# GDN gates held in their SBUF buffers until the mLSTM gate adds them, and rows of x asked for one step sooner

## The chip, the cores and the metric

The kernel runs on one core of a Trainium2 chip. Five engines work side by side, each through its own queue in order: TensorE (PE, whose weight loads are shown apart as PEld), VectorE (DVE), ScalarE (ACT), GpSimd (POOL) and SyncE (SP), which issues the DMAs here. The metric is the device time in microseconds. Three runs of the kernel before took 1170.3, 1171.71 and 1173.52 us; the median, 1171.71, is the time before.

## The reference

One decoder layer with two groups of heads side by side, for a prompt of 1024 tokens (behind 16 learned meta tokens) and 8 sample tokens with cached state; D_MODEL is 1024:

```python
# x <- x + W_out [ mLSTM_group(h) ; GDN_group(h) ],  h = RMSNorm(x)
# all head inputs from one projection h @ W_in; every branch has a SiLU gate path;
# a final RMSNorm is applied
M_HEADS, M_DK, M_DV = 4, 128, 256       # mLSTM, matrix memory
G_HEADS, G_DK, G_DV = 8, 128, 128       # gated DeltaNet
```

Outputs are the rows y for prompt and sample, and the new states of both groups. What the change touches is the end of it: each head's result (normalised, in 128-wide pieces, eight of the mLSTM group and eight of the GDN group) is multiplied by its gate and enters the product with W_out, whose result is added to x.

## The kernel before, in words

**Stages.** First come the projections and the chunked recurrences. Each head's normalised result is left in DRAM as `h_d[k]`, 128 x 1024 per piece: k = 0 to 7 are mLSTM pieces and 8 to 15 GDN heads. The gate values z of the GDN heads stand in `g_d`. From about 800 us on TensorE computes the gates of the mLSTM pieces: for j = 0 to 7 one job `o{j}` and one `zm{j}`, each in three blocks of 344 columns (in texts: o1_0, o1_1, o1_2, zm1_0 ...) of 24 matmuls (three for each of eight slices of D: high by high, low by high, high by low). A block goes to one of two PSUM banks in turn. An o block is emptied by a tanh on ScalarE (`to`), a zm block by a tanh on ScalarE (`thzm`) and two operations on VectorE (`mg<-thzm,pjzm`, which frees the bank, and `mg<-to,mg`). Splits of weights into high and low parts run between (`who`, `whzm` on ScalarE, `wlo`, `wlzm` on VectorE).

**Gates.** Both kinds of gate are one generator, `gate` (L1691). For a GDN piece (number 8 + j) it loads y from `g_d` and ht from `h_d`, multiplies them (`y<-ht,wgh,y`, four operations on VectorE), stores y to `y_d` in DRAM, makes the high and low part of its first half for the left operand of the first output product (`left<-y`, `left<-y,left`), and stores the difference of its halves in `s_d`. For mLSTM piece j it loads ht, multiplies it with the gate mg (`mg<-ht,wmq,mg`, four operations), loads the y of GDN piece j back from `y_d` as `yg`, forms two sums (`ht<-mg,yg`), another sum and a difference (`yg<-yg,mg`, `yg<-mg`), and stores five pieces in `c_d`. Buffers come from the ring `r_gm`, which has five here; `r_gm.can()` says whether one is free.

**Output products.** The product with W_out is done as seven products (`out_products`), 0 to 6, of sums and differences of halves (a scheme of Strassen's kind: s_d and c_d hold the left sums, `owh`/`owl` the right ones). Each has four banks t = 0 to 3 and steps k = 0 to 7, 96 matmuls of 512 columns; product p begins a bank when the drain of product p - 2 has emptied it. A drain (`drain`) adds a bank to the rows of x, which it finds in the buffers `regionxl` (three pieces) and `xr1_1`, `xr0_2`, `xr1_2`, `xr0_3`, `xr1_3`. `residual` (L2059) asks for these rows from DRAM; `("used", p, k)` is noted when product p's step k has been written for its last bank.

**Order.** A planner (`Plan`) sets the order of the work. Each part of the program is a generator that yields what it waits for; the planner keeps an estimated clock per engine and estimated times at which tiles are written and read, takes the next part by them and records the instruction on its engine. All instructions are recorded by one helper, so that every row of the profile shows L56. The sample tokens' head (`small`, `mqT`, `mqc`, `wb`, `mms`) is woven between the gate jobs by the same planner: `mqT` turns a row on TensorE, `mqc` are its small products, after which GpSimd multiplies two 128 x 1024 states by a decay (`small<-small,sgb`), the six `wb` operations of 8 elements are its weights, and `mms` begins a chain of some twenty operations of 32 elements (`wb`, ending in `hs`), a Newton iteration for its norm.

Of the kernel before, what the change touches and what calls it, by code (L numbers as in the profile page):

```python
# [12 lines left out]
F32 = mybir.dt.float32  # L13
# [294 lines left out]
def hymba_kernel(ctx: ExitStack, tc: tile.TileContext, a: dict, o: dict):  # L308
# [1365 lines left out]
    y_d = dr.tile([GH, P, SEQ], F32, name="y_d")  # L1674
    s_d = dr.tile([GH, P, HALF], F32, name="s_d")
    c_d = dr.tile([GH, P, 5, HALF], F32, name="c_d")
    for t, size in ((y_d, P * SEQ), (s_d, P * HALF), (c_d, 5 * P * HALF)):
        plan.split(t, size)
# [12 lines left out]
    def gate(kt_, wcol):  # L1691

        j = kt_ % 8
        if kt_ >= 8:
            yield lambda: ("mP", MH - 1) in done and ("H", kt_) in done and ("z", j) in done and (j in slots or (r_kq if j < 6 else r_N).can()) and r_gm.can(2)
            gi, y = r_gm.get([SEQ], f"y{kt_}")
        else:
            yield lambda: ("H", kt_) in done and ("y", 8 + j) in done and (j < 2 or ("y", j - 2) in done) and r_gm.can()
        hi, ht = r_gm.get([8, P], f"ht{kt_}")
        yield max(plan.read[ht.tensor.name], plan.read[y.tensor.name] if kt_ >= 8 else 0.0)  # L1700
        if kt_ >= 8:
            sp.dma_start(y, g_d[j])
        sp.dma_start(ht.rearrange("p c t -> p (c t)"), h_d[kt_])
        yield ht
        if kt_ < 8:
            yield has("zm", j)
            gi, y = hd["mg", j]
        yield y
        if kt_ < 8:
            act.activation(gs[:, j, :], y[:, SEQ:NO], AF.Copy, scale=wcol)  # L1710
        u = ht.rearrange("p c t -> p (c t)")
        for a_ in range(4):
            yield "dve"
            to = y[:, 0:SEQ].rearrange("p (c a i) -> p a c i", c=8, a=4)[:, a_]
            dve.scalar_tensor_tensor(out=to, in0=u[:, 256 * a_ : 256 * a_ + 256].rearrange("p (c i) -> p c i", c=8), scalar=wcol, in1=to, op0=ALU.mult, op1=ALU.mult)
        yield y
        if kt_ >= 8:
            sp.dma_start(y_d[j], y)
            high, low = slot(j)
            act.copy(high, y[:, 0:HALF])  # L1720
            dve.tensor_tensor(out=u[:, 0:HALF], in0=y[:, HALF:SEQ], in1=y[:, 0:HALF], op=ALU.subtract)
            yield high
            dve.tensor_tensor(out=low, in0=y[:, 0:HALF], in1=high.bitcast(F32), op=ALU.subtract)
            r_gm.free(gi)
            yield u
            sp.dma_start(s_d[j], u[:, 0:HALF])
            r_gm.free(hi)
        else:
            sp.dma_start(c_d[j, :, 0], y[:, HALF:SEQ])
            yield r_gm.can  # L1730
            yi, g = r_gm.get([SEQ], f"yg{j}")
            yield plan.read[g.tensor.name]
            sp.dma_start(g, y_d[j])
            yield g
            for half in (slice(0, HALF), slice(HALF, SEQ)):
                yield "dve"
                dve.tensor_tensor(out=u[:, half], in0=y[:, half], in1=g[:, half], op=ALU.add)
            yield "dve"
            dve.tensor_tensor(out=g[:, 0:HALF], in0=g[:, 0:HALF], in1=y[:, HALF:SEQ], op=ALU.add)
            yield "dve"  # L1740
            dve.tensor_tensor(out=g[:, HALF:SEQ], in0=y[:, 0:HALF], in1=y[:, HALF:SEQ], op=ALU.subtract)
            r_v.free(gi)
            yield g
            sp.dma_start(c_d[j, :, 1:3], u.rearrange("p (a t) -> p a t", a=2))
            r_gm.free(hi)
            sp.dma_start(c_d[j, :, 3:5], g.rearrange("p (a t) -> p a t", a=2))
            r_gm.free(yi)
# [544 lines left out]
```

## Time and profile before

| | |
|---|---|
| median of three runs | 1171.71 us (1170.3 to 1173.52) |
| the profiled execution, in all | 1170.97 us |
| its span, first to last instruction | 1169.2 us |
| mean granted TensorE clock | 0.998 |
| PE / PEld / DVE / ACT / POOL busy | 1151.9 / 1079.4 / 910.6 / 587.8 / 467.6 us |
| DMA | 171.63 MB, mean 147 GB/s |

In timelines a row has start, duration (of one, or over a group xN), engine, line, operation, out<-in, shape, and in brackets the idle time before it with what ended it. In the table of stretches a row has the stretch, its length, busy time (and instructions) of PE, PEld, DVE, ACT and POOL, the granted clock, the DMA engines' share and GB/s. Matmuls overlap in the pipeline: one of 344 columns lasts 0.32 us in a row, and the next starts 0.157 us after it. A wait's row names the waiting engine and tile, the engine and tile that ended the wait, the total, the count and the longest.

### The profile page before, as it was taken

The page shows a single profiled execution, that of the slowest core. Times are in us where ns is not written, and L with a number is a line of the kernel's source. Part 1 is how long each engine was busy: PE and PEld are TensorE (multiplying, and loading weights), DVE is VectorE, ACT ScalarE, POOL GpSimd, SP SyncE. Part 2 cuts the span into 40 slices and gives each one's busy share as a digit, 9 for nine tenths or more (in the row PEclk, how much of TensorE's full clock was granted, in tenths as well). Part 3 has the DMA queues.
Part 4 walks back from the last instruction along what each step waited for, and adds up shares of the span by engine and source line. Part 5 has one row for each costly group of instructions (what it writes and reads, how often), then busy time and mean ns, then how long its engine had stood idle before and what let it go on. Part 6 is the DMA issues. An engine that isn't in the chain of part 4 may idle for free.

```text
span 1169.2 us, 22728 instructions
## 1 busy us (share of the span) xinstructions
PE 1151.9 (99%) x8049; PEld 1079.4 (92%) x8049; DVE 910.6 (78%) x2324; ACT 587.8 (50%) x1814; POOL 467.6 (40%) x644
## 2 busy tenths in 40 slices
PE   8999999999999999999999999999999999999997
PEld 7999999999999999999999998999999999876885
DVE  6789878698787879887664967677877765997896
ACT  6544445565655565745454546466532222433443
POOL 3104877855738285958411451311111000530012
PEclk9999999999999999999999999999999999999999
DMA  6032311322121223022423294677998888673342
GB/s 249 18 100 71 95 51 50 102 60 88 46 83 62 81 64 88 26 67 83 120 79 107 70 338 142 244 236 252 297 361 284 303 296 312 214 263 121 107 155 88
DMA packets 94461, 171.63 MB, mean 147 GB/s; under 512 B 28026, under 2 KB 53842, under 8 KB 94347
## 3 DMA queue, kind: packets, MB, share of 16 engines
q1 hardware_dynamic: 94152, 170.01, 44.2%
q8 instruction: 63, 1.03, 0.3%
q14 instruction: 52, 0.42, 0.1%
q10 hardware_dynamic: 194, 0.17, 0.0%
HBM read 116.04 MB, written 54.10 MB: 146 GB/s over the span
## 4 chain that ended last, share of the span: by engine, by line
PE 85%; DMA 6%; DVE 5%; issue 2%; ACT 1%; SPq 1%; POOL 0%; DVEq 0%; ACTq 0%
PE pjg L56 24%; PE pjm L56 15%; PE op L56 9%; PE pjz L56 8%; PE pjo L56 5%; PE pjzm L56 4%; PE up L56 4%; PE tp L56 3%; PE sk L56 2%; PE mnm L56 2%; PE mup L56 2%; PE kk L56 1%; DMA out_s_C<-small 1%; DMA s_d<-ht 1%; DMA ht<-h_d 1%
## 5 line engine op out<-in xcount | busy, mean ns | idle before, releaser
L56 PE MATMUL pjg<-xht,whg 128*128 128x350 f32 (+6 forms) x624 | 197.4, 323 | 1.0 <-ACT xht L56 1.0
L56 PE MATMUL pjg<-xlt,whg 128*128 128x350 f32 (+6 forms) x624 | 196.8, 322 | 0.0
L56 PE MATMUL pjg<-xht,wlg 128*128 128x350 f32 (+6 forms) x592 | 190.3, 325 | 0.0
L56 POOL TENSOR_TENSOR tmp<-B,E 33x31 f32<-33x31 f32 (+15 forms) x248 | 146.2, 590 | 70.9 <-DMA B<-nd 52.1
L56 POOL TENSOR_TENSOR E<-E,tmp 33x31 f32<-33x31 f32 (+15 forms) x248 | 155.5, 627 | 19.4
L56 PE MATMUL op<-owh,left 128*128 128x512 f32 x448 | 141.5, 395 | 2.4 <-DVE xr L56 2.4
L56 PE MATMUL pjm<-xht,whm 128*128 128x350 f32 (+2 forms) x384 | 127.1, 331 | 0.0
L56 PE MATMUL pjm<-xht,wlm 128*128 128x350 f32 (+2 forms) x384 | 126.4, 329 | 0.0
L56 PE MATMUL pjm<-xlt,whm 128*128 128x350 f32 (+2 forms) x384 | 125.4, 327 | 0.0
L56 PEld LDWEIGHTS pjg<-xht,whg 128*128 128x128 f32 x624 | 116.4, 189 | 1.6 <-issue 1.2
L56 PEld LDWEIGHTS pjg<-xlt,whg 128*128 128x128 f32 x624 | 116.4, 189 | 0.4
L56 PEld LDWEIGHTS pjg<-xht,wlg 128*128 128x128 f32 x592 | 110.9, 189 | 0.5
L56 PEld LDWEIGHTS op<-owh,left 128*128 128x128 f32 x448 | 84.1, 188 | 24.8 <-DVE xr L56 3.3
L56 DVE SCALAR_TENSOR_TENSOR kq<-cr,prm,kq 128x346 f32<-128x346 f32 (+7 forms) x147 | 97.2, 667 | 10.8 <-ACT cr L56 8.0
L56 PE MATMUL op<-owl,left 128*128 128x512 f32 x224 | 88.5, 395 | 0.0
L56 PEld LDWEIGHTS pjm<-xht,wlm 128*128 128x128 f32 x384 | 72.4, 189 | 0.5 <-issue 0.2
L56 PEld LDWEIGHTS pjm<-xht,whm 128*128 128x128 f32 x384 | 72.4, 188 | 0.5 <-issue 0.2
L56 PEld LDWEIGHTS pjm<-xlt,whm 128*128 128x128 f32 x384 | 72.4, 188 | 0.5 <-issue 0.2
L56 ACT COPY cr<-pjg 128x3 f32<-128x3 f32 (+8 forms) x124 | 40.5, 327 | 51.3 <-PE pjg L56 50.9
L56 PE MATMUL pjo<-xht,who 128*128 128x344 f32 x192 | 61.9, 322 | 2.3 <-ACT to L56 1.5
L56 PE MATMUL pjz<-xht,wlz 128*128 128x344 f32 x192 | 62.8, 327 | 0.0
L56 PE MATMUL pjz<-xht,whz 128*128 128x344 f32 x192 | 62.8, 327 | 0.0
(377 smaller groups left out, 3095.3 us busy)
## 6 DMA issues: line engine op xcount, KB each, us to landing
wrg<-in_wt SPq DMA_DIRECT2D x23, 512.0 KB, 3.6
left<-c_d SPq DMA_DIRECT2D x40, 256.0 KB, 2.7
wrm<-in_wt SPq DMA_DIRECT2D x16, 512.0 KB, 6.0
h_d<-turn SPq DMA_DIRECT2D x64, 128.0 KB, 3.9
ht<-h_d SPq DMA_DIRECT2D x16, 512.0 KB, 9.3
gm<-rows_d SPq DMA_DIRECT2D x8, 576.0 KB, 5.5
xt<-in_x_p SPq DMA_DIRECT2D x8, 512.0 KB, 5.0
wrz<-in_wt SPq DMA_DIRECT2D x8, 512.0 KB, 3.3
```

Source lines behind the costliest of these rows:

```text
L56: r = f(*args, **kw)
```

## The change

GDN gates and mLSTM gates become two generators that share `scaled`. A GDN gate no longer stores y to DRAM; it keeps its buffer in `hd["y", j]`, and the mLSTM gate of the same number takes it from there, forms the sums in it, and frees it after the store to `c_d`. A GDN gate from number 2 on now starts only when the mLSTM gate two numbers earlier is done, a condition that stood on the mLSTM gate before. `y_d` is gone, with its eight stores and eight loads. In `residual` the rows of x for t = 2 are asked for when product 1 has used step 0 (before: step 1), and those for t = 3 when it has used step 1 (before: step 2).

```diff
--- before.py
+++ after.py
@@ -1671,10 +1671,9 @@
     ys = gp.tile([P, 20, NS], F32, name="ys")
     wgh = gp.tile([P, 1], F32, name="wgh")
     wmq = gp.tile([P, 8], F32, name="wmq")
-    y_d = dr.tile([GH, P, SEQ], F32, name="y_d")
     s_d = dr.tile([GH, P, HALF], F32, name="s_d")
     c_d = dr.tile([GH, P, 5, HALF], F32, name="c_d")
-    for t, size in ((y_d, P * SEQ), (s_d, P * HALF), (c_d, 5 * P * HALF)):
+    for t, size in ((s_d, P * HALF), (c_d, 5 * P * HALF)):
         plan.split(t, size)
     slots = {}
     def slot(k):
@@ -1688,64 +1687,64 @@
                 slots[k + i] = t[:, i, 0], t[:, i, 1]
         return slots[k]
 
-    def gate(kt_, wcol):
-
-        j = kt_ % 8
-        if kt_ >= 8:
-            yield lambda: ("mP", MH - 1) in done and ("H", kt_) in done and ("z", j) in done and (j in slots or (r_kq if j < 6 else r_N).can()) and r_gm.can(2)
-            gi, y = r_gm.get([SEQ], f"y{kt_}")
-        else:
-            yield lambda: ("H", kt_) in done and ("y", 8 + j) in done and (j < 2 or ("y", j - 2) in done) and r_gm.can()
-        hi, ht = r_gm.get([8, P], f"ht{kt_}")
-        yield max(plan.read[ht.tensor.name], plan.read[y.tensor.name] if kt_ >= 8 else 0.0)
-        if kt_ >= 8:
-            sp.dma_start(y, g_d[j])
-        sp.dma_start(ht.rearrange("p c t -> p (c t)"), h_d[kt_])
-        yield ht
-        if kt_ < 8:
-            yield has("zm", j)
-            gi, y = hd["mg", j]
-        yield y
-        if kt_ < 8:
-            act.activation(gs[:, j, :], y[:, SEQ:NO], AF.Copy, scale=wcol)
-        u = ht.rearrange("p c t -> p (c t)")
+    def scaled(y, ht, wcol):
+
         for a_ in range(4):
             yield "dve"
             to = y[:, 0:SEQ].rearrange("p (c a i) -> p a c i", c=8, a=4)[:, a_]
-            dve.scalar_tensor_tensor(out=to, in0=u[:, 256 * a_ : 256 * a_ + 256].rearrange("p (c i) -> p c i", c=8), scalar=wcol, in1=to, op0=ALU.mult, op1=ALU.mult)
+            h_ = ht[:, 256 * a_ : 256 * a_ + 256].rearrange("p (c i) -> p c i", c=8)
+            dve.scalar_tensor_tensor(out=to, in0=h_, scalar=wcol, in1=to, op0=ALU.mult, op1=ALU.mult)
         yield y
-        if kt_ >= 8:
-            sp.dma_start(y_d[j], y)
-            high, low = slot(j)
-            act.copy(high, y[:, 0:HALF])
-            dve.tensor_tensor(out=u[:, 0:HALF], in0=y[:, HALF:SEQ], in1=y[:, 0:HALF], op=ALU.subtract)
-            yield high
-            dve.tensor_tensor(out=low, in0=y[:, 0:HALF], in1=high.bitcast(F32), op=ALU.subtract)
-            r_gm.free(gi)
-            yield u
-            sp.dma_start(s_d[j], u[:, 0:HALF])
-            r_gm.free(hi)
-        else:
-            sp.dma_start(c_d[j, :, 0], y[:, HALF:SEQ])
-            yield r_gm.can
-            yi, g = r_gm.get([SEQ], f"yg{j}")
-            yield plan.read[g.tensor.name]
-            sp.dma_start(g, y_d[j])
-            yield g
-            for half in (slice(0, HALF), slice(HALF, SEQ)):
-                yield "dve"
-                dve.tensor_tensor(out=u[:, half], in0=y[:, half], in1=g[:, half], op=ALU.add)
+
+    def gdn_gate(j):
+
+        yield lambda: ("mP", MH - 1) in done and ("H", 8 + j) in done and ("z", j) in done and (j in slots or (r_kq if j < 6 else r_N).can()) and r_gm.can(2) and (j < 2 or ("y", j - 2) in done)
+        gi, y = r_gm.get([SEQ], f"y{8 + j}")
+        hi, u = r_gm.get([SEQ], f"ht{8 + j}")
+        yield max(plan.read[u.tensor.name], plan.read[y.tensor.name])
+        sp.dma_start(y, g_d[j])
+        sp.dma_start(u, h_d[8 + j])
+        yield u
+        yield y
+        yield from scaled(y, u, wgh)
+        high, low = slot(j)
+        act.copy(high, y[:, 0:HALF])
+        dve.tensor_tensor(out=u[:, 0:HALF], in0=y[:, HALF:SEQ], in1=y[:, 0:HALF], op=ALU.subtract)
+        yield high
+        dve.tensor_tensor(out=low, in0=y[:, 0:HALF], in1=high.bitcast(F32), op=ALU.subtract)
+        yield u
+        sp.dma_start(s_d[j], u[:, 0:HALF])
+        r_gm.free(hi)
+        hd["y", j] = gi, y
+        done.add(("y", 8 + j))
+
+    def gate(j, wcol):
+
+        yield lambda: ("H", j) in done and ("y", 8 + j) in done and r_gm.can()
+        hi, u = r_gm.get([SEQ], f"ht{j}")
+        yield plan.read[u.tensor.name]
+        sp.dma_start(u, h_d[j])
+        yield u
+        yield has("zm", j)
+        (vi, y), (gi, g) = hd["mg", j], hd["y", j]
+        yield y
+        act.activation(gs[:, j, :], y[:, SEQ:NO], AF.Copy, scale=wcol)
+        yield from scaled(y, u, wcol)
+        sp.dma_start(c_d[j, :, 0], y[:, HALF:SEQ])
+        for half in (slice(0, HALF), slice(HALF, SEQ)):
             yield "dve"
-            dve.tensor_tensor(out=g[:, 0:HALF], in0=g[:, 0:HALF], in1=y[:, HALF:SEQ], op=ALU.add)
-            yield "dve"
-            dve.tensor_tensor(out=g[:, HALF:SEQ], in0=y[:, 0:HALF], in1=y[:, HALF:SEQ], op=ALU.subtract)
-            r_v.free(gi)
-            yield g
-            sp.dma_start(c_d[j, :, 1:3], u.rearrange("p (a t) -> p a t", a=2))
-            r_gm.free(hi)
-            sp.dma_start(c_d[j, :, 3:5], g.rearrange("p (a t) -> p a t", a=2))
-            r_gm.free(yi)
-        done.add(("y", kt_))
+            dve.tensor_tensor(out=u[:, half], in0=y[:, half], in1=g[:, half], op=ALU.add)
+        yield "dve"
+        dve.tensor_tensor(out=g[:, 0:HALF], in0=g[:, 0:HALF], in1=y[:, HALF:SEQ], op=ALU.add)
+        yield "dve"
+        dve.tensor_tensor(out=g[:, HALF:SEQ], in0=y[:, 0:HALF], in1=y[:, HALF:SEQ], op=ALU.subtract)
+        r_v.free(vi)
+        yield g
+        sp.dma_start(c_d[j, :, 1:3], u.rearrange("p (a t) -> p a t", a=2))
+        r_gm.free(hi)
+        sp.dma_start(c_d[j, :, 3:5], g.rearrange("p (a t) -> p a t", a=2))
+        r_gm.free(gi)
+        done.add(("y", j))
 
     def silu_evac(name, g, to=None):
         def evac(pt, c0, n):
@@ -1811,7 +1810,7 @@
 
     def gdn_gates():
         for h in range(GH):
-            yield from gate(8 + h, wgh)
+            yield from gdn_gate(h)
 
     def gate_jobs():
         def tile_(key, name):
@@ -2060,7 +2059,7 @@
         yield has("region")
         for h in (1, 0):
             for t in range(4):
-                yield has("used", 2 - h, t - (t > 1) if h else t)
+                yield has("used", 2 - h, t // 3 if h else t)
                 for c in range(2):
                     if h:
                         n = 2 * t + c
```

The planner's order is the same on all engines up to about the block zm0_1. Three places where it differs follow, as the queues stand.

VectorE around the evacuation of the block zm0_2 (`pjzm0_2` is its bank, `y9`/`ht9` GDN gate 9, `ebuf` and `wb` the sample head). Before:

```order
L56 SCALAR_TENSOR_TENSOR mg0_10741<-thzm0_360_10852,pjzm0_1_10805 128x344
L56 SCALAR_TENSOR_TENSOR mg0_10741<-to0_10372,mg0_10741 128x344
L56 TENSOR_TENSOR wlo1_10815<-wro1_10338,who1_10814 128x256
L56 SCALAR_TENSOR_TENSOR y9_10735<-ht9_10736,wgh_166,y9_10735 128x8x32 x4
L56 SCALAR_TENSOR_TENSOR ebuf0_101<-ebuf1_102,wb_105,ebuf0_101 128x128 x2
L56 SCALAR_TENSOR_TENSOR mg0_10741<-thzm0_704_10897,pjzm0_2_10856 128x344
```

And now:

```order
L56 SCALAR_TENSOR_TENSOR mg0_10738<-thzm0_360_10856,pjzm0_1_10803 128x344
L56 SCALAR_TENSOR_TENSOR mg0_10738<-to0_10371,mg0_10738 128x344
L56 TENSOR_TENSOR wlo1_10813<-wro1_10337,who1_10812 128x256
L56 SCALAR_TENSOR_TENSOR y9_10733<-ht9_10734,wgh_166,y9_10733 128x8x32 x2
L56 TENSOR_TENSOR wb_105<-mqT0_10851,sgb_97 128x8
L56 TENSOR_TENSOR wb_105<-wb_105,msam_160 128x8
L56 TENSOR_TENSOR wb_105<-wb_105 128x8
L56 TENSOR_TENSOR wb_105<-mqT0_10851,sgb_97 128x8
L56 TENSOR_TENSOR wb_105<-wb_105,msam_160 128x8
L56 TENSOR_TENSOR wb_105<-wb_105 128x8
L56 SCALAR_TENSOR_TENSOR y9_10733<-ht9_10734,wgh_166,y9_10733 128x8x32 x2
L56 SCALAR_TENSOR_TENSOR mg0_10738<-thzm0_704_10921,pjzm0_2_10860 128x344
```

The six `wb` operations have moved in ahead of the evacuation: on TensorE `mqT` now stands between zm0_1 and zm0_2 and `mqc` behind 12 matmuls of zm0_2, where before both stood in o1_1.

VectorE around the sample head's Newton chain, with `mms` on TensorE (before in o5_1, now in o4_2 behind 12 of its 24 matmuls). Before:

```order
L56 SCALAR_TENSOR_TENSOR wb<-mms,wb 128x32
L56 TENSOR_SCALAR wb<-wb 128x32
L56 TENSOR_TENSOR wb<-wb 128x32 x2
L56 TENSOR_SCALAR wb<-wb 128x32
L56 TENSOR_TENSOR wb<-wb 128x32
L56 TENSOR_TENSOR wlzm_12041<-wrzm_11837,whzm_12040 128x384
L56 TENSOR_TENSOR wb<-wb 128x32 x2
L56 TENSOR_SCALAR wb<-wb 128x32
L56 TENSOR_TENSOR wb<-wb 128x32
L56 TENSOR_TENSOR wlzm_12041<-wrzm_11837,whzm_12040 128x384
```

And now, from the chain's end on:

```order
L56 TENSOR_TENSOR wb<-wb 128x32 x3
L56 TENSOR_SCALAR wb<-wb 128x32
L56 TENSOR_TENSOR wb<-wb 128x32
L56 TENSOR_TENSOR hs<-wb 128x4x8 x2
L56 SCALAR_TENSOR_TENSOR mg_11600<-ht_11729,wmq,mg_11600 128x8x32 x3
L56 TENSOR_TENSOR ht_11729<-mg_11600,y_11477 128x512 x2
L56 TENSOR_TENSOR y_11477<-y_11477,mg_11600 128x512
L56 TENSOR_TENSOR y_11477<-mg_11600 128x512
L56 SCALAR_TENSOR_TENSOR mg_11888<-thzm_16_11922,pjzm_0_11889 128x344
```

The chain has no weight splits in it any more; three products and four sums of mLSTM gate 3 follow it, and then the evacuation of zm4_0.

VectorE in the drains of products 0 and 1 (`op0_3` is product 0's bank 3). Before:

```order
L56 TENSOR_TENSOR xr1_2_12904<-xr1_2_12904,op0_2_12701 128x512
L56 TENSOR_TENSOR regionxl_12684<-regionxl_12684,op1_0_12852 128x512
L56 TENSOR_TENSOR xr1_1_12900<-xr1_1_12900,op1_1_12861 128x512
L56 TENSOR_TENSOR xr0_3_12922<-xr0_3_12922,op0_3_12705 128x512
L56 TENSOR_TENSOR left2_11101<-left2_11101 128x512
L56 TENSOR_TENSOR xr1_3_12924<-xr1_3_12924,op0_3_12705 128x512
```

And now:

```order
L56 TENSOR_TENSOR xr1_2_12858<-xr1_2_12858,op0_2_12678 128x512
L56 TENSOR_TENSOR left0_10693<-left0_10693 128x512
L56 TENSOR_TENSOR xr0_3_12879<-xr0_3_12879,op0_3_12682 128x512
L56 TENSOR_TENSOR owl0_12565<-regionxl_12661,owh0_12564 128x512 x2
L56 TENSOR_TENSOR xr1_3_12881<-xr1_3_12881,op0_3_12682 128x512
L56 TENSOR_TENSOR regionxl_12661<-regionxl_12661,op1_0_12831 128x512
L56 TENSOR_TENSOR xr1_1_12854<-xr1_1_12854,op1_1_12836 128x512
```

Both drains of bank 3 of product 0 now stand ahead of two drains of product 1 and of a split of a left slot (`left2`).

## The prediction

> **What bounds the kernel now.** I read the busy shares first, then TensorE's waits over the stretch in which the change acts, then the three stretches as a table.
>
> ```profile
> span 1169.2 us, 22728 instructions
> PE 1151.9 (99%) x8049; PEld 1079.4 (92%) x8049; DVE 910.6 (78%) x2324; ACT 587.8 (50%) x1814; POOL 467.6 (40%) x644
> ...
> PE op L56 <- DVE xr L56: 2.4, 2, 2.0
> PE pjo L56 <- ACT to L56: 1.5, 1, 1.5
> PE pjo L56 <- DVE mg L56: 0.8, 1, 0.8
> PE pjzm L56 <- DVE mg L56: 0.2, 1, 0.2
> ...
> 800.00:1000.00 200.00, 197.42 (x1312) 192.74 (x1311) 149.75 (x374) 71.60 (x206) 23.97 (x11) 1.00 0.86 300
> 1000.00:1045.00 45.00, 42.56 (x183) 33.64 (x182) 43.90 (x51) 16.91 (x30) 21.14 (x8) 1.00 0.73 257
> ```
>
> TensorE is busy for all but 17.3 of 1169.2 us. From 780 us to the end its waits (the four rows; total us, times, longest) come to 2.4 + 1.5 + 0.8 + 0.2 = 4.9 us, and the rest of its idle time lies before that stretch and behind its last matmul, which the change leaves alone. No matmul is removed. So 4.9 us, 0.42% of the span, is all that can be won, whatever is taken off the queues. The window rows (PE, PEld, DVE, ACT, POOL, clock, DMA share, GB/s) show where slack is thin: DMA engines 86% busy in the gate stretch, VectorE 43.90 of 45 us busy in the drains.
>
> The five waits have two kinds of cause. Three are in the gate stretch, the two long ones of which are these:
>
> ```profile
> 952.54 1.67 DVE L56 SCALAR_TENSOR_TENSOR y<-ht,wgh,y 128x256 f32<-128x256 f32 x4 [4.71 <-DMA ht<-h_d]
> 955.28 0.43 PE L56 MATMUL pjo<-xht,who 128*128 128x344 f32 x1 [1.52 <-ACT to L56]
> 968.74 1.67 DVE L56 SCALAR_TENSOR_TENSOR y<-ht,wgh,y 128x256 f32<-128x256 f32 x4 [3.56 <-DMA ht<-h_d]
> 971.36 0.42 PE L56 MATMUL pjo<-xht,who 128*128 128x344 f32 x1 [0.76 <-DVE mg L56]
> ```
>
> VectorE waits 4.71 us for a GDN gate's state. ScalarE's cast of that gate's y waits for VectorE, and the tanh that empties a projection bank (to) is queued behind the cast, so TensorE loses 1.52. The next wait is 3.56 and costs 0.76. In both places TensorE forgives about 3 us (4.71 - 1.52 = 3.19; 3.56 - 0.76 = 2.80) and then pays one for one. The other two waits are in the first two output products:
>
> ```profile
> 1041.18 0.50 PE L56 MATMUL op<-owh,left 128*128 128x512 f32 x1 [0.41 <-DVE xr L56]
> 1043.44 1.27 DVE L56 TENSOR_TENSOR xr<-xr,op 128x512 f32<-128x512 f32 x2
> 1044.17 0.50 PE L56 MATMUL op<-owh,left 128*128 128x512 f32 x1 [2.03 <-DVE xr L56]
> ```
>
> Product 2 needs the banks of product 0, whose last drain VectorE finishes in the x2 group at 1043.44 (0.60 us apiece), too late by 2.03.
>
> **The change part by part.** First the round trip through DRAM.
>
> ```profile
> y_d<-y SPq DMA_DIRECT2D x8, 512.0 KB, 3.7
> yg<-y_d SPq DMA_DIRECT2D x8, 512.0 KB, 5.5
> ...
>   DMA yg<-y_d: 6.9, 3
> ```
>
> Sixteen transfers of 512 KB go, 8.4 MB; all eight pairs sit between 800 and 1015 us, where 300 GB/s times 200 us is 60 MB, so about a seventh of that stretch's traffic. VectorE loses three waits of 6.9 us together (the last row, from the tile yg). None of those three is at one of the five places where TensorE waits, so they give nothing directly. They give room on VectorE. No vector, scalar or GpSimd operation is added or removed; SP issues 16 fewer.
>
> For the gate-phase waits, 1.52 + 0.76 + 0.18 = 2.46 us: the state loads have a seventh less traffic against them, which speaks for their going. Against it: a GDN gate's buffer is now held until the mLSTM gate of its number has stored its sums, so the loads of gates 12 to 15 stand behind stores out of the very buffers that they fill, where before the first store released them. Bounds: all 2.46 gained, or none. I take 1.5, so that 1.0 stays: the traffic is sure to go, and the release has room in the mean (the held buffers, below).
>
> The drain waits, 0.41 + 2.03 = 2.44 us: product 0's last drain moves ahead of three other vector operations, 3 x 0.60 = 1.8 us, and an idle piece in front of the last gate goes:
>
> ```profile
> 1014.24 0.69 DVE L56 TENSOR_TENSOR ht<-mg,yg 128x512 f32<-128x512 f32 x1 [0.93 <-DVE owl L56]
> ...
> 1024.84 2.23 SPq L56 DMA_DIRECT2D xr<-in_x_p  x3
> ...
> 1029.38 0.99 SPq L56 DMA_DIRECT2D xr<-in_x_p  x2
> ```
>
> 1.8 + 0.93 = 2.7 us, more than the 2.03 and the 0.41. The rows of x asked for one k step sooner cost nothing: two DMA groups move up in SP's queue past one weight load, and there is no new transfer. With the old times they were issued at 1024.84 and 1029.38 and wanted from about 1038 on, so their own lateness isn't a term; what they do is let the planner write the drains earlier. Bounds: all 2.44, or none if VectorE, 98% busy there, only trades one late operation for another. I take all.
>
> Now what the new order puts in the way. The sample head's turning and its mqc products move from the block o1_1 into zm0_2 on TensorE; with them six small wb operations move in among gate 8's, and GpSimd's pair of products starts there.
>
> ```profile
> 823.16 0.32 PE L56 MATMUL pjzm<-xht,whzm 128*128 128x344 f32 x1
> 826.92 0.32 PE L56 MATMUL pjo<-xht,who 128*128 128x344 f32 x1
> 831.94 0.60 PE L56 MATMUL mqT<-ident,srow 128*128 128x128 f32 x4
> 834.35 1.08 PE L56 MATMUL mqc<-small,msam 128*32 128x128 f32 x32
> 835.11 4.11 POOL L56 TENSOR_TENSOR small<-small,sgb 128x1024 f32<-128x1024 f32 x2 [14.90 <-PE mqc L56]
> 835.56 1.81 DVE L56 TENSOR_TENSOR wb<-wb,msam 128x8 f32<-128x8 f32 x1
> 837.40 1.84 DVE L56 TENSOR_TENSOR wb<-wb 128x8 f32<-128x8 f32 x1
> ```
>
> While GpSimd runs its two 2.05 us products, a vector operation with two operands in SBUF waits for the end of one of them: 1.81 and 1.84 us for what takes 0.16 otherwise (the row at 900.02, below). About one gets through per product. Placed in zm0_2: the block starts at 823.16; the turning (0.60) and 12 matmuls of 0.157 ((826.92 - 823.16)/24) bring mqc to 825.6; GpSimd starts 0.76 later (834.35 to 835.11), 826.4, and ends at 826.4 + 4.11 = 830.5. VectorE's queue then:
>
> ```profile
> 826.39 0.42 DVE L56 TENSOR_TENSOR wlo<-wro,who 128x256 fp32r<-128x256 f32 x1
> 826.72 1.67 DVE L56 SCALAR_TENSOR_TENSOR y<-ht,wgh,y 128x256 f32<-128x256 f32 x4
> 828.83 0.51 DVE L56 SCALAR_TENSOR_TENSOR mg<-thzm,pjzm 128x344 f32<-128x344 f32 x1
> ...
> 900.02 0.16 DVE L56 TENSOR_TENSOR wb<-mqT,sgb 128x8 f32<-128x8 f32 x1
> 900.70 1.78 DVE L56 TENSOR_TENSOR wb<-wb 128x8 f32<-128x8 f32 x1
> ```
>
> After wlo and one y product have got through, three y products (3 x 0.40) and the six wb (900.02 to 0.17 past 900.70, 0.85 when free) are left: 830.5 + 1.2 + 0.85 = 832.55, and the evacuation of zm0_2 (0.51) ends at 833.1. TensorE reaches o1_1, which wants that bank, at 826.92 + 0.60 + 1.08 (mqc) + 24 x 0.157 = 832.4; before, it got there at 830.7, and the evacuation had ended at 829.3. A new stall of 0.7, and 0.3 of hand-over: 1.0 us. Bounds: 0 where the operations don't collide, and 2.0 where one more y product is left (0.4) and GpSimd starts later, or TensorE's insertions take less than their rows (0.6).
>
> The Trainium skill, "SBUF — State Buffer", section Who interferes with whom, has a vector operation with two SBUF inputs blocked fully by a GpSimd operation that reads SBUF, and one with a single SBUF input not held at all. By that the evacuation, which reads PSUM too, isn't itself held, and the stall comes only from what is queued before it, as in the sum; if it were held as well, the stall would be the same, since its turn comes after 830.5. The rows at 835.56 and 837.40 agree with the blocking.
>
> The second place is the Newton chain for the sample's norms. Before, it stood among weight splits in o5_1; now it stands in o4_2 in one piece, and three mg products and four gate sums follow it, ahead of the evacuation of zm4_0.
>
> ```profile
> 928.04 0.53 PE L56 MATMUL mms<-wb,ones 128*128 128x32 f32 x4
> 928.61 0.19 DVE L56 SCALAR_TENSOR_TENSOR wb<-mms,wb 128x32 f32<-128x32 f32 x1 [1.40 <-PE mms L56]
> 928.83 1.99 DVE L56 TENSOR_SCALAR wb<-wb 128x32 int32<-128x32 int32 x1
> 934.23 0.29 DVE L56 TENSOR_TENSOR hs<-wb 128x32 f32<-128x32 f32 x2
> ...
> 862.17 1.29 DVE L56 TENSOR_TENSOR ht<-mg,yg 128x512 f32<-128x512 f32 x2 [1.93 <-DMA yg<-y_d]
> ```
>
> From the start of mms: 0.57 to the chain, the chain 5.9 less two splits of 0.47 = 5.0 (a blocked 1.99 in it), products 1.2, sums 2.5 (two in 1.29), evacuation 0.5, hand-over 0.2: 10.0 us. TensorE wants the bank after mms 0.5, 12 matmuls 1.9, and two blocks 7.5: 9.9. So 0.1 late with the blocked piece in it and 1.7 early without; bounds 0 and 1.9 (one more blocked operation). I take 0.4.
>
> Sum: -2.4 - 1.5 + 1.0 + 0.4 = -2.5 us. The profiled execution took 1170.97 in all (1.8 around its span); 1170.97 - 2.5 = 1168.5. The runs' median of 1171.71 lies 0.74 above that execution, so 1169.2 on the runs' terms.
>
> **The rivals.** *All old waits go, no new one comes:* -4.9, 1166.1 on the profiled execution, 1166.8 on the median. For it: less traffic, no added work. Against it: the two new places above have no cover left by their own rows.
>
> *Slower, the held buffers:* GDN gates 12 to 15 load only after a store from their buffer has landed, and VectorE's queue is in order, with the evacuations of two banks behind each y product. It decides once VectorE waits more than about 3 us in such a place. The landing times of the tile ht in this stretch, and a store's:
>
> ```profile
> DMA to landing us min/median/max: 4.1/5.8/9.3
> ...
> c_d<-ht SPq DMA_DIRECT2D x8, 512.0 KB, 4.1
> ```
>
> If the four states take 9.3 us rather than 5.8, the waits of 3.6 to 4.7 grow toward 5.5 and more: 4 x 2.5 us of TensorE = 10, less the 4.9 that go, +5.1: 1176.1 on the profiled execution, 1176.8 on the median. Against it: a gate's period is six blocks of 3.77, 22.6 us, and store plus load need 4.1 + 9.3 = 13.4 of it.
>
> *The change does nothing that counts:* in the drains VectorE is saturated, so a drain moved up puts the split of a weight or of a left slot behind it, and TensorE waits there for 2.4 all the same; the gate waits change places. Within 1 us of 1171.7.
>
> *TensorE has more to give than its waits show.* Weight loads are busy 192.74 of 200 us in the gate stretch, 7.3 idle, where matmuls leave 2.6. If matmul rows hid idle time, the stretch could give 4.7 us more, 1164.5. Against it: the matmuls start every 0.157 us on both sides of a stall, so nothing is hidden between them. The Trainium skill, "Perfetto Trace Analysis", section Identifying the Most-Contended Engine, says that busy matmuls are no measure and busy weight loads are; here the constant pace decides against reading the difference as slack.
>
> **How the numbers follow.** A measurement of this kernel can tell about 0.3%, 3.5 us, from no change. The forecast (a gain of 1 to 3.5 us) has 0.42; nothing that counts (within 1 us, or a little slower) 0.16; all waits gone, with no more than a small new one 0.25, of which most is past 3.5 us; more than the waits 0.03; slower by the buffers 0.14, of which 0.13 is past 3.5 us. That gives faster by over 0.3%: 0.27; within: 0.60; slower: 0.13. The range goes from 1166 (all waits gone, 0.8 below) to 1174 (the new stalls at their upper bounds, 2.0 + 1.9, with the gate waits unchanged and the drains' 2.4 gone, is +1.5, 1173.2; half of the slower case, +2.5, is 1174.2).
>
> **What would show it.** Right: TensorE's waits after 780 us fall to about 2.5 us; the two waits on xr are gone; a wait on mg appears at the start of o1_1, near 832, with a vector operation stretched to some 1.8 us under GpSimd's pair just before it; no group yg. Wrong: waits above 5 us; y products on VectorE waiting over 3 us for ht in gates 12 to 15 with pjo or pjzm waits behind them (the slower case); a clock below 1.00 in the table of stretches; or a span that moves by more than TensorE's waits do.

## The result and the profile after

The changed kernel took 1164.54 us in the median of five runs (1163.84 to 1165.14), the kernel before 1170.30 (1168.59 to 1173.52, five runs): a ratio of 0.9947, with a 95% interval of 0.9930 to 0.9965. That is 0.5% faster. The forecast was 1169.2 in a range of 1166 to 1174, so the direction was right, the size fell short by more than half (2.5 us forecast, 5.8 measured), and the time lies 1.5 us below the range. Of the 4.7 us between 1169.2 and 1164.54, 1.4 are the baseline's: the median of the kernel before was 1171.71 over three runs and is 1170.30 over five. A second set of runs of the same kernel gave 0.9948 (0.9930 to 0.9966). Over all runs the changed kernel stayed between 1163.8 and 1165.1 us, while the kernel before went from 1166.6 to 1175.7, so the change took out scatter too. Three executions that lie far off (2282.76 and 2282.91 us of the kernel before, 4247.08 of one experiment) are left out throughout.

The busy shares, TensorE's waits from 780 us on, and the two stretches of the changed kernel, in the columns of before:

```profile
span 1163.3 us, 22690 instructions
PE 1150.6 (99%) x8049; PEld 1079.3 (93%) x8049; DVE 909.1 (78%) x2324; ACT 588.3 (51%) x1814; POOL 468.6 (40%) x644
...
PE pjo L56 <- DVE mg L56: 0.5, 1, 0.5
PE pjzm L56 <- DVE mg L56: 0.2, 1, 0.2
...
800.00:1000.00 200.00, 199.31 (x1324) 194.63 (x1323) 153.22 (x378) 73.58 (x209) 23.55 (x11) 1.00 0.75 260
1000.00:1045.00 45.00, 45.00 (x196) 36.37 (x195) 44.83 (x55) 18.48 (x32) 21.99 (x8) 1.00 0.77 266
```

All five old waits are gone, 4.9 us, and TensorE is busy for the whole of the drains' stretch (45.00 of 45 us, before 42.56); two new waits of 0.50 and 0.18 us have come. In the gate stretch the DMA engines' share fell from 0.86 to 0.75 and the rate from 300 to 260 GB/s, which is the seventh of the traffic that the prediction counted.

The first new wait is the one at o1_1, where the prediction had put it. TensorE's and VectorE's timelines there:

```profile
823.38 0.60 PE L56 MATMUL mqT<-ident,srow 128*128 128x128 f32 x4
825.79 1.08 PE L56 MATMUL mqc<-small,msam 128*32 128x128 f32 x32
832.39 0.32 PE L56 MATMUL pjo<-xht,wlo 128*128 128x344 f32 x1
833.22 0.42 PE L56 MATMUL pjo<-xht,who 128*128 128x344 f32 x1 [0.50 <-DVE mg L56]
833.48 0.32 PE L56 MATMUL pjo<-xlt,who 128*128 128x344 f32 x1
...
826.54 3.98 POOL L56 TENSOR_TENSOR small<-small,sgb 128x1024 f32<-128x1024 f32 x2 [6.12 <-PE mqc L56]
826.60 2.15 DVE L56 TENSOR_TENSOR wlo<-wro,who 128x256 fp32r<-128x256 f32 x1
828.67 2.53 DVE L56 SCALAR_TENSOR_TENSOR y<-ht,wgh,y 128x256 f32<-128x256 f32 x2
831.87 0.88 DVE L56 SCALAR_TENSOR_TENSOR y<-ht,wgh,y 128x256 f32<-128x256 f32 x2
832.66 0.51 DVE L56 SCALAR_TENSOR_TENSOR mg<-thzm,pjzm 128x344 f32<-128x344 f32 x1
```

GpSimd's pair holds VectorE's queue (wlo 2.15 instead of 0.42 us), and the evacuation starts at 832.66 (worked out beforehand: 832.55).

The same rows show what a wait costs. From 832.39 to 833.22 are 0.83 us, where the next matmul is otherwise due after 0.157: 0.67 lost, though the wait's own row says 0.50. The matmul after the wait holds up its successor for 0.26 instead of 0.157, another 0.10. So a wait of 0.50 loses 0.78. The long wait of before shows the same surcharge in its timeline:

```profile
953.44 0.32 PE L56 MATMUL pjo<-xht,wlo 128*128 128x344 f32 x1
955.28 0.43 PE L56 MATMUL pjo<-xht,who 128*128 128x344 f32 x1 [1.52 <-ACT to L56]
955.54 0.32 PE L56 MATMUL pjo<-xlt,who 128*128 128x344 f32 x1
```

1.84 - 0.157 = 1.68, and 0.26 - 0.157 = 0.10 behind it: 1.78 us for a row of 1.52. Matmuls overlap in the pipeline, and a wait counts only from where the last one has drained. Counted so, from start to start, the five old waits cost 6.2 us and not 4.9.

The accounts of the two profiled executions (1170.97 and 1165.14, 5.8 apart): old waits -6.2; new waits +0.78 and +0.44; a hitch of 0.40 in front of a pjzm matmul that before had and no wait row names (matmuls start at 918.24, 918.68 and 918.95, where 0.157 is due each time); the time from the last matmul's start to the end of the span 8.15 before and 7.75 after, 0.4, which is the landing of the last rows of y. Sum -5.8.

### The profile page after: what moved, and what is told of

Read it like the earlier page. It is cut to its first block, busy times and chain, and to the rows that moved or that the text cites. A ratio compares the mean times of both kernels' runs of the same rounds, so it can differ in the third digit from the quotient of the medians.

```text
span 1163.3 us, 22690 instructions
## 1 busy us (share of the span) xinstructions
PE 1150.6 (99%) x8049; PEld 1079.3 (93%) x8049; DVE 909.1 (78%) x2324; ACT 588.3 (51%) x1814; POOL 468.6 (40%) x644
## 4 chain that ended last, share of the span: by engine, by line
PE 90%; DVE 5%; DMA 2%; ACT 1%; issue 1%; POOL 0%; SPq 0%; DVEq 0%
PE pjg L56 23%; PE pjm L56 15%; PE op L56 13%; PE pjz L56 8%; PE pjo L56 5%; PE pjzm L56 5%; PE up L56 4%; PE tp L56 3%; PE sk L56 2%; PE mnm L56 2%; PE mup L56 2%; PE kk L56 1%; PE W L56 1%; PE xtp L56 1%; PE E L56 1%
## 5 line engine op out<-in xcount | busy, mean ns | idle before, releaser
L56 PE MATMUL pjz<-xlt,whz 128*128 128x344 f32 x192 | 62.7, 326 | 0.0
```

The source lines that it names most:

```text
L56: r = f(*args, **kw)
```

## The experiments

Three questions stood open: which part of the change brought the gain, whether it came from the order of the queues or from the traffic, and what makes the new wait. All experiments keep the planner's order row for row where they say so: an instruction that is added or left out is hidden from the planner, and one that is shrunk is shown to it at its old size. In the tables of waits the columns are the engine and tile, what ended the wait, us in total, times, longest; where VectorE waits, the stretch is 800 to 1020 us. Ratios are to the kernel before on the same chip, with 95% intervals.

**Each part alone.** Gates alone: the changed kernel with

```diff
-                yield has("used", 2 - h, t // 3 if h else t)
+                yield has("used", 2 - h, t - (t > 1) if h else t)
```

> The held buffers alone, with the rows of x asked for at the old steps; its queues are those of the changed kernel but for 6 rows of VectorE and 9 of SP in the drains. Theory A, each edit mends its own place: the three waits of the gate stretch stay away (1.52 + 0.76 + 0.18 us and about 0.26 us of restart each, 3.2 us) and the two waits on xr come back (2.44 + 0.5 = 2.9 us), so about 2.9 us slower than the changed kernel: ratio to before near 0.9972. Theory B, the gates mend both, since the drains get the idle time that the last gate's readback held: no wait on xr over 0.2 us, ratio within 0.0005 of 0.9947 to 0.995.

Rows alone: the kernel before with the reverse of that line.

> The kernel before with only the rows of x asked for one step sooner; TensorE's order is that of before, VectorE's differs by 11 rows in the drains. Theory A: both waits on xr go or shrink below 0.3 us together, the three gate waits stay, ratio near 0.9975. Theory B: the waits on xr stay at 1.5 us or more in total, ratio 0.999 to 1.000.

Gates alone took 1165.71 us, 0.9944 (0.9927 to 0.9961): the whole gain. Rows alone took 1168.60, 0.9978 (0.9963 to 0.9992). TensorE's waits of the two, gates alone first:

```profile
PE mup L56 <- ACT va L56: 0.9, 1, 0.9
PE pjo L56 <- DVE mg L56: 0.5, 1, 0.5
PE mup L56 <- ACT mjk L56: 0.3, 1, 0.3
```

```profile
PE pjo L56 <- ACT to L56: 2.2, 1, 2.2
PE op L56 <- DVE xr L56: 1.7, 1, 1.7
PE op L56 <- DVE left L56: 0.6, 1, 0.6
PE pjzm L56 <- DVE mg L56: 0.2, 1, 0.2
```

With the gates alone no wait on xr is left (the two mup waits lie at 795 and 802 us, before the gates). Theory B holds: the gates mend the drains too. With the rows alone 1.7 of the 2.4 us on xr stay, and 0.6 comes on a left slot instead. The ratio is near theory A's 0.9975, the trace near theory B's. So by the times the rows alone do help somewhat on the kernel before; this trace, of an execution that was the slowest of its twelve (1171.77), doesn't show where. On top of the gates nothing of the rows can be seen: 1165.71 against 1164.54, on different chips, with 1163.66 the lowest of the one and 1163.84 of the other.

**Traffic or order.** The traffic put back into the changed kernel, order kept, nobody waiting for it:

```diff
         yield from scaled(y, u, wgh)
+        nc.sync.dma_start(y_d[j], y)
...
         sp.dma_start(c_d[j, :, 0], y[:, HALF:SEQ])
+        nc.sync.dma_start(y2_d[j], y_d[j])
```

> The changed kernel with its order kept row for row on TensorE, VectorE, ScalarE and GpSimd, and the traffic put back on SP: each GDN gate's y is stored to DRAM as before, and where the readback stood a copy of 512 KB from DRAM to DRAM is issued; nobody waits for it. Theory traffic (the loads of the states land sooner because 8.4 MB less go): ht lands in 5 us or more in the median again instead of 3.5, waits of 1.5 us or more appear on TensorE in the gate stretch, ratio 0.9965 or above. Theory order (what counts is what stands where, and that no operation waits for a readback): TensorE's waits stay at about 0.7 us, ratio 0.994 to 0.9955.

And taken out of the kernel before, order kept:

```diff
-            sp.dma_start(y_d[j], y)
+            nc.sync.dma_start(y_d[j, :, 0:64], y[:, 0:64])
...
-            sp.dma_start(g, y_d[j])
+            nc.sync.dma_start(g[:, 0:64], y_d[j, :, 0:64])
...
```

> The kernel before, order kept row for row, with the round trip of y cut to 32 KB each way in place of 512 KB (the sums read only these 64 columns, so they leave out the rest of y and the output isn't the reference's). Theory traffic: the three gate waits (1.52, 0.76, 0.18 us) go, ratio near 0.997; the waits on xr stay at about 2.4 us, less what the earlier yg of the last gate gives back (up to 0.9). Theory order: the gate waits stay within 0.5 us of 2.46 in total, ratio 0.999 to 1.0005.

With the traffic back the changed kernel took 1170.33 us, 0.9986 (0.9971 to 1.0000): nearly all of the gain is gone, with the new order and the held buffers in place. With the trip cut to 32 KB the kernel before took 1166.37, 0.9952 (0.9935 to 0.9970): nearly all of the gain, with the old order. The list of TensorE's waits after 780 us is empty in its trace: the waits on xr are gone too, of which theory traffic had left 1.5 us or more. TensorE's waits and the gate stretch with the traffic back, and then VectorE's waits for state loads with it cut:

```profile
PE pjo L56 <- DVE mg L56: 1.6, 2, 1.1
PE pjzm L56 <- DVE mg L56: 1.5, 1, 1.5
...
800.00:1000.00 200.00, 196.94 (x1312) 192.53 (x1311) 148.53 (x377) 71.88 (x206) 23.35 (x11) 1.00 0.86 300
```

```profile
DVE y L56 <- DMA ht<-h_d: 2.8, 2, 2.3
```

With the traffic back the stretch is again at 0.86 and 300 GB/s, the states (ht) land in 7.2 us in the median instead of the changed kernel's 3.5, and TensorE waits 2.4 us longer for evacuations in it (3.1 against 0.7). So the bytes alone, with no vector operation waiting for the readback, bring gate waits back, and the new order doesn't keep them away. What a late load costs hangs on its place: in the changed kernel, too, VectorE waits 9.7 us for states (5.2 for `mg<-ht`, 4.5 for `y<-ht`), and TensorE loses 0.7. Three limits: the put-back copies go from DRAM to DRAM, which also writes 4.2 MB that the old readback didn't, so this is at least the old traffic, and the profiled execution (1168.62) was quicker than the median, so its waits show only part of the loss; and cutting the trip shortens the traffic, the wait for the readback itself and whatever waits for the store of y.

**Which half, and does the place matter.** Only the store put back, only a copy in the readback's place (from `g_d`), and sixteen copies of 512 KB from rows of x, issued between about 250 and 650 us:

```diff
...
+    def elsewhere():
+        for h in range(GH):
+            yield has("C", h)
+            for i in range(2):
+                nc.sync.dma_start(y2_d[2 * h + i], a["x_p"][P * h : P * h + P])
...
```

> The changed kernel, order kept, with only the eight stores of y to DRAM put back (4.2 MB), nobody waiting for them. Both halves of the traffic together brought the ratio from 0.9947 to 0.9986. If bytes count alike: about half of that, 0.9965, ht landing at 5 us in the median. If the store hardly counts (it runs right behind the y products, when the state is already there): 0.995 or less and ht at 4 us or less.

> The changed kernel, order kept, with only the eight readbacks' traffic put back, as 512 KB copies from DRAM to DRAM (4.2 MB read, 4.2 MB written) where the readback stood. If bytes count alike: about 0.9965. If the readback is the half that collides (it stands in the queue right by the loads of the next states): 0.998 or above, and the store alone near 0.995.

> The changed kernel, order kept, with sixteen copies of 512 KB from DRAM to DRAM (of rows of x) issued between about 250 and 650 us, where the DMA engines are 20 to 45% busy. Theory (traffic costs only where the loads of the states are due, 800 to 1000 us): ratio as the changed kernel, 0.994 to 0.9955, no new wait on TensorE. Rival (any 8.4 MB more cost by themselves): 0.997 or above.

On one chip: elsewhere 1164.92 us, 0.9959 (0.9945 to 0.9973); store only 1166.19, 0.9969 (0.9958 to 0.9979); copy only 1166.37 (1164.14 to 1168.13), 0.9972 (0.9961 to 0.9983; no trace of it is read). On that chip the kernel before was low, 1169.33, which lifts all three ratios (the first lies just above its theory's 0.9955); against the traffic elsewhere the store costs 1.3 us and the copy 1.5. Each half counts, and neither makes the whole; I had given the copy a chance to be the one that collides, and these runs don't tell the two apart. As many bytes in the middle of the program cost nothing that can be seen, and bring no new wait on TensorE. Its stretches, to show that the bytes are there (28% and 25% and 27% of the DMA engines in the changed kernel's first three, which become 28, 31 and 31):

```profile
200.00:400.00 200.00, 199.79 (x1656) 192.64 (x1655) 161.54 (x453) 117.42 (x399) 121.89 (x197) 1.00 0.31 94
400.00:600.00 200.00, 199.84 (x1610) 191.73 (x1609) 156.36 (x412) 113.61 (x374) 129.52 (x204) 1.00 0.31 95
800.00:1000.00 200.00, 199.50 (x1324) 194.83 (x1323) 153.18 (x376) 72.67 (x205) 24.92 (x12) 1.00 0.75 263
```

**Where the drain waits came from.** The traffic doesn't explain them: with it put back no wait on xr returns. What is left is the last gate's readback, for which VectorE and, behind it, SP's stores wait. The kernel before with the trip cut for the last gate alone (`j == 7`), and for all the others (`j < 7`), of which this is the readback's part:

```diff
-            sp.dma_start(g, y_d[j])
+            if j == 7:
+                nc.sync.dma_start(g[:, 0:64], y_d[j, :, 0:64])
+            else:
+                sp.dma_start(g, y_d[j])
```

> The kernel before, order kept, with the round trip of the last gate's y alone cut to 32 KB each way (that gate's sums read 64 columns only, so the output isn't the reference's). Theory two places (the waits on xr come from the last gate's readback, those in the gate stretch from the traffic of the others): the waits on xr shrink from 2.4 us to under 0.5, the gate waits stay, ratio 0.9975 to 0.9985. Theory one cause (all of it is the traffic of the gate stretch): the waits on xr stay above 1.5 us, ratio 0.999 or above.

> The kernel before, order kept, with the round trips of gates 0 to 6 cut to 32 KB and the last one left whole (output not the reference's for those). Theory two places: the gate waits (2.46 us) go, the waits on xr stay near 2.4, ratio 0.997 to 0.998. Theory one cause: all five waits go, ratio as with all eight cut, 0.995 or less.

The last trip cut: 1168.04 us, 0.9982 (0.9968 to 0.9996). The first seven cut: 1168.42, 0.9980 (0.9965 to 0.9995). Together that is 0.38%, of the 0.48% that cutting all eight gave (0.9952), well within the intervals. TensorE's waits and VectorE's for the states, first with the last trip cut (an execution of 1170.26 us, slower than the median):

```profile
PE pjo L56 <- ACT to L56: 1.6, 1, 1.6
PE pjo L56 <- DVE mg L56: 1.3, 1, 1.3
PE pjzm L56 <- DVE mg L56: 0.9, 3, 0.5
...
DVE y L56 <- DMA ht<-h_d: 9.5, 3, 4.8
```

Then with the first seven cut:

```profile
PE op L56 <- DVE xr L56: 2.8, 2, 2.0
...
DVE y L56 <- DMA ht<-h_d: 1.4, 1, 1.4
```

Each cut takes its own kind of wait away and leaves the other. So there are two places: the trips of gates 0 to 6 cost in the gate stretch (VectorE's wait for the states is 9.5 us with them and 1.4 without), the trip of gate 7 in the drains.

In the gate stretch the bytes have their part, by the runs with traffic put back. A second path isn't separated from them. SP's queue, too, waits for the stores of y to land, in the kernel before between 800 and 1000 us:

```profile
SPq L56 <- DMA y_d<-y: 15.0, 4, 5.9
```

The longest, 5.9 us, stands right ahead of two loads issued at 945.66 and 946.26 us; the second is the state for which VectorE then waits 4.71 us and TensorE 1.52. With the first seven trips cut these waits are 7.9 us in two places, and the changed kernel has none. The run with all the traffic back has none either and still shows gate waits, so the bytes suffice for them (the mere issuing of the transfers doesn't: it stays where the trip is cut to 32 KB, and the gain is there); no run keeps these waits without the bytes, and their share of the 0.20% stays open.

The last trip reaches the drains by the wait for the readback and not by its bytes, since its bytes put back bring no wait on xr. SP's and VectorE's timelines of before and after; the first output product starts at 994.50 and at 992.17 us:

```profile
1010.09 0.42 SPq L56 DMA_DIRECT2D yg<-y_d  x1
1016.65 2.89 DVE L56 TENSOR_TENSOR yg<-mg 128x512 f32<-128x512 f32 x1
1019.57 0.32 SPq L56 DMA_DIRECT2D c_d<-yg  x1
1021.62 0.94 SPq L56 DMA_DIRECT2D regionxl<-in_x_p  x2
```

```profile
1012.19 0.32 SPq L56 DMA_DIRECT2D c_d<-y  x1
1017.93 1.37 SPq L56 DMA_DIRECT2D regionxl<-in_x_p  x3
1036.28 0.68 DVE L56 TENSOR_TENSOR xr<-xr,op 128x512 f32<-128x512 f32 x1
```

And with the last trip alone cut, where the product starts at 996.45:

```profile
1017.70 2.89 DVE L56 TENSOR_TENSOR yg<-mg 128x512 f32<-128x512 f32 x1
1020.62 0.32 SPq L56 DMA_DIRECT2D c_d<-yg  x1
1042.74 1.27 DVE L56 TENSOR_TENSOR xr<-xr,op 128x512 f32<-128x512 f32 x2
```

Before, the store of the last sums is issued 25.1 us after the product's start; after, 20.0. The last drain of product 0 ends at 1036.28 + 0.68, 44.8 us after the start, where before it was 1044.1 (the first of the x2 group at 1043.44), 49.6 after. These 4.8 us are nearly twice the 2.7 that the prediction counted. With the last trip alone cut the store is issued 24.2 us after the start, and the drain ends at 1043.4 (the first of the x2 group), 47.0 after it. So the readback makes 0.9 of the 5.1 us at the store, which is the idle 0.93 of before, and 2.6 of the 4.8 at the drain, and that is enough for the waits on xr to go (a hitch of 0.3 us at 1043 that no wait row names is left). The last sum is held for 2.89 us with the trip cut as well, so this hold isn't the readback's. The other 2.2 us came with the changed kernel; what makes them up isn't shown.

**The new wait.** GpSimd's pair left out at that one place, order kept:

```diff
-                pool.tensor_tensor(out=sb[i], in0=sb[i], in1=decb[:, h].unsqueeze(2).to_broadcast([P, NS, P]), op=ALU.mult)
+                decay = decb[:, h].unsqueeze(2).to_broadcast([P, NS, P])
+                if h == 1:
+                    plan.note("pool", "tensor_tensor", sb[i], [sb[i], decay], None, False)
+                else:
+                    pool.tensor_tensor(out=sb[i], in0=sb[i], in1=decay, op=ALU.mult)
```

> The changed kernel, order kept, with GpSimd's one pair of 128x1024 decays behind the mqc in zm0_2 left out (two sample states aren't decayed, so the output isn't the reference's). Theory lock (the vector operations queued ahead of zm0_2's evacuation are held by this pair): the wait of 0.50 us at o1_1 goes, wlo and the y products there take 0.42 and 0.48 us again, and the matmuls lose 0.78 us less in all (0.50 + 0.28 of restart); ratio to before about 0.0007 below the changed kernel's, which the times alone can't tell. Rival (the six wb operations alone are too many): the wait stays at 0.3 us or more.

1163.64 us (1163.53 to 1164.13), 0.9952 (0.9936 to 0.9967) on the chip on which the kernel with its traffic elsewhere took 1164.92. VectorE's timeline there:

```profile
825.28 0.42 DVE L56 TENSOR_TENSOR wlo<-wro,who 128x256 fp32r<-128x256 f32 x1
825.61 0.88 DVE L56 SCALAR_TENSOR_TENSOR y<-ht,wgh,y 128x256 f32<-128x256 f32 x2
827.16 0.87 DVE L56 SCALAR_TENSOR_TENSOR y<-ht,wgh,y 128x256 f32<-128x256 f32 x2
828.16 0.51 DVE L56 SCALAR_TENSOR_TENSOR mg<-thzm,pjzm 128x344 f32<-128x344 f32 x1
```

The operations take their free times again and the evacuation starts at 828.16 instead of 832.66: TensorE doesn't wait there. (A wait of 0.2 us on a mg evacuation comes at another place.) The lock is the cause.

A version meant to beat both kernels issues the decays of all mLSTM states in quarters, and the planner reorders for it:

```diff
             for i in range(2):
-                pool.tensor_tensor(out=sb[i], in0=sb[i], in1=decb[:, h].unsqueeze(2).to_broadcast([P, NS, P]), op=ALU.mult)
+                for b in range(0, NS, 2):
+                    pool.tensor_tensor(out=sb[i][:, b : b + 2], in0=sb[i][:, b : b + 2], in1=decb[:, h, b : b + 2].unsqueeze(2).to_broadcast([P, 2, P]), op=ALU.mult)
```

> The changed kernel with GpSimd's decays of the mLSTM states issued in quarters (128x256, four to a state) instead of one operation of 128x1024, so that a vector operation waits for 0.7 us at most and one passes between any two. Theory lock: the wait of 0.50 us at o1_1 goes (VectorE's seven operations ahead of the evacuation pass in about 4 us while the eight quarters run, and the evacuation ends before 832), 0.8 us fewer for the matmuls; the planner reorders some 130 rows of VectorE for it, so another wait may come. Time 0.5 to 1 us below the changed kernel's, which only its narrow spread could show. Rival: eight shorter holds cost as much as two long ones, and the wait stays at 0.3 us or more.

> The changed kernel once more, unaltered, beside the next three on one chip: ratio 0.993 to 0.9965, TensorE's waits after 780 us under 1 us in total.

Side by side: quarters 1164.79 us (1164.02 to 1165.97), the changed kernel 1164.62 (1164.22 to 1164.89). The wait at o1_1 shrank to 0.17 us, since VectorE's operations got through between the quarters:

```profile
825.62 5.44 POOL L56 TENSOR_TENSOR small<-small,sgb 128x256 f32<-128x256 f32 x8 [5.87 <-PE mqc L56]
828.82 0.54 DVE L56 TENSOR_TENSOR wb<-wb 128x8 f32<-128x8 f32 x1
831.67 0.50 DVE L56 SCALAR_TENSOR_TENSOR mg<-thzm,pjzm 128x344 f32<-128x344 f32 x1
```

It is the only wait of TensorE that is left in this profile after 780 us, and the times don't show the difference. It is no better kernel by these runs.

## Why the prediction was right or wrong

**Right:** what bounds the kernel, and by which five waits; the direction; the place, the mechanism and nearly the size of the wait at o1_1 (1.0 us forecast; 0.50 in the row, 0.78 with its restart; the hand-over of 0.3 that the forecast added was 0.05); that both waits on xr go; that the clock stays at 1.00.

**Wrong, the first step: "4.9 us, 0.42% of the span, is all that can be won".** The step took the rows of waits for the loss. From start to start the five waits cost 6.2 us, about 0.27 more each than their rows. That cap kept the whole distribution of the forecast too high: of the 3.3 us between the forecast sum (-2.5) and the profiled executions (-5.8), 1.3 lie here and 0.4 in the hitch at 918 us, which has no row among the waits at all. (The others: 1.0 in the next step, 0.2 in the new waits, 1.2 instead of 1.4, and 0.4 in the last rows' landing.) The rule "a wait row is a lower bound" could have been found in the trace of before, in the starts just ahead of and behind the wait that was quoted.

**Wrong, the second: "I take 1.5, so that 1.0 stays" of the gate waits.** All 2.46 went (3.2 with restarts), and only 0.18 came in that stretch beside the one at o1_1. A state that comes late, which is what held me back, is there in one place of the changed kernel:

```profile
938.48 1.68 DVE L56 SCALAR_TENSOR_TENSOR mg<-ht,wmq,mg 128x256 f32<-128x256 f32 x4 [5.16 <-DMA ht<-h_d]
943.16 0.42 PE L56 MATMUL pjzm<-xht,whzm 128*128 128x344 f32 x1 [0.18 <-DVE mg L56]
```

VectorE waits 5.16 us for a state and TensorE loses 0.18, 0.44 with the restart. Whether the load was late because it had to wait for a store out of its buffer or because of other traffic wasn't tried. The "about 3 us" that TensorE forgives held for the two places it was read from; here it was 5. So the rival *slower, the held buffers* would have needed longer waits than it assumed.

**Mis-sized: the Newton chain, 0.4 us.** It cost nothing. VectorE's chain ran in one piece with no operation blocked (0.18 us for the one that had taken 1.99), which was the 1.7 us early of the prediction's own sum, and the price taken lay between the two cases.

**Right in size, wrong in cause: the drains.** The 2.4 us (2.97 with restarts) went, but the order that the earlier rows of x make is not needed for it: with the gates alone they go, with the rows alone most of them stay. The last gate's readback is enough: the idle 0.93 in front of its sums, counted there as a small extra, was the visible part of the cause, and with this one trip cut the drains end 2.6 us earlier.

**Wrong: the weight given to the traffic.** "None of those three is at one of the five places where TensorE waits, so they give nothing directly" was true of VectorE's waits for readbacks, and the prediction then let the seventh less of traffic be an argument for 1.5 us. The runs make the first seven trips, whose bytes were thought of little worth, 0.20% of the 0.53%, with 0.18% from the last trip; and all the traffic put back, in its heavier form, takes all but 0.14%.

**The rivals.** *All old waits go, no new one comes* came nearest, and still gave 1166.8 against 1164.54 (1166.1 against 1165.14 for the profiled executions), by the cap of 4.9 and the higher baseline. *The change does nothing that counts* and *slower* fall. *TensorE has more to give than its waits show* was argued from weight loads and dismissed by the constant pace on both sides of a stall. The pace is constant, and within the stall the difference is there: it was put at no more than 3 in 100 for a reason that looked beside the place. Its size, 4.7 us, is not borne out; 1.7 is (1.3 of restarts, 0.4 at 918 us).

The Trainium skill's rule, "SBUF — State Buffer", section Who interferes with whom, is borne out for the operations with two operands in SBUF: with GpSimd's pair left out they run at their free times. Its other half, that an operation with one operand there isn't held, wasn't put to the test for the evacuation, whose turn came after the pair. The Trainium skill excepts the two-port modes from that half, which the prediction left out, and the kernel before has a row that may be such a case: a TENSOR_SCALAR of 128x32 with one operand took 1.99 us at 928.83, while GpSimd ran from 928.40 to 930.79, and 0.18 in the changed kernel with GpSimd idle.

## What to carry to other kernels

Count a stall of TensorE from matmul start to matmul start and not from its wait row: with pipelined matmuls the row leaves out the drained pipeline, here about 0.27 us a time, 1.3 of the 3.3 us by which the profiled execution went past the forecast. A round trip through DRAM costs in two ways that need separate tests: by its traffic wherever other loads are due with no cover, and by its latency at the one place where nothing else is left to do; the first is found by putting the bytes back with nobody waiting for them, the second by cutting one trip. Look at the queue that issues the loads, too: a store that it waits for (5.9 us here) holds every load behind it. In the middle of the program, at a DMA share of 0.31, as many bytes cost nothing that the times show.

## What the runs showed of the hardware

A transfer that no compute engine waits for can still cost them time: eight stores of 512 KB more in some 200 us (DMA share 0.80, the states landing in 5.6 us in the median instead of 3.5) cost 1.3 us, eight copies 1.5, stores and copies together (0.86, 7.2 us) 4.6 by the ratios, and sixteen copies at a share of 0.3 nothing that can be seen. The scatter grows with it in part: twelve runs with the traffic back lie within 5.5 us, eleven with stores only within 3.0, five and six of the changed kernel within 1.3 and 0.7. But six of the gates alone, which have the changed kernel's traffic, lie within 2.9, and six of the kernel before with the trip cut within 3.8, so the traffic isn't all that makes it.
